# A two-layer hybrid encoder on one core: weight sums moved from VectorE to accumulating DMA, products of the MLP's first half in another order

## The chip, the core and the metric

The kernel runs on one core of a Trainium2 chip. Its engines work from queues of their own and wait for one another by semaphores: PE (TensorE) multiplies, DVE (VectorE) and ACT (ScalarE) do elementwise work, POOL (GpSimd) does a few small operations and issues DMA, and SP (SyncE) issues DMA. The metric is the time of one execution on the device, in microseconds.

## The reference

The reference is an encoder of two layers on one sequence of 512 positions with 1024 features, all in float32. Cut to what matters here:

```python
for l in range(DEPTH):
    xn = rms_norm(x, ln1[l])
    z = xn @ w_in[l]
    a_q, a_i, a_ff, a_fb, a_g, b_u, b_v, c_q, c_k, c_v, gz = jnp.split(z, offsets, axis=-1)
    ...   # branch A: gated scans; B: spatial gating; C: windowed attention
    merged = (gates[:, :, 0] * (y_a @ w_br[l, 0])
              + gates[:, :, 1] * (y_b @ w_br[l, 1])
              + gates[:, :, 2] * (y_c @ w_br[l, 2]))
    x = x + merged @ w_out[l]
    hn = rms_norm(x, ln2[l])
    x = x + jnp.square(jax.nn.relu(hn @ w_up[l])) @ w_down[l]
return rms_norm(x, final_norm)
```

`w_up` is 1024 x 4096 and `w_down` 4096 x 1024, in each layer.

## The kernel before

**Products in float32.** Every operand is split in two: `hi`, a cast of it, and `lo`, what the cast leaves. A product is three matmuls, hi by hi, hi by lo and lo by hi. For weights the cast runs on ACT (`wsplit`, L271, writes `wh`) and the rest is formed on DVE (L272, writes `wl`). Weights come in chunks of 128x1024, 512 KB. There are three buffers each of `wh` and `wl`, so a chunk can be split only when PE has finished with the chunk three places earlier. Activations are split in the same way (L336 on ACT, L337 on DVE).

**Seven products instead of eight.** The larger multiplications are cut into 2x2 blocks and done with seven block products, for which sums of weight blocks and sums of activation blocks are needed. A unit has seven products, each of two weight chunks, so fourteen splits. The blocks of a weight are called b11, b12, b22 and b21.

**The units of the MLP.** The hidden features are cut into four quarters (`qd`). For each quarter there is an `up` unit and then a `down` unit, a pair. Both run through `block_products`, in the order 1, 7, 6, 2, 5, 4, 3 (`ORDER`). The tile `t3` holds b12; b22 is added to it by an accumulating DMA issued by POOL (L261), for product 7. After that DVE adds b11 to it for product 6, and after product 6 it adds b21 for product 4 (both L548). b11 gets b12 by an accumulating DMA after product 7, for product 5. The result of product 1 is copied by ACT into a second pair of banks (`m`), so that product 2 accumulates on it there. The output of `up` goes through a squared ReLU and is split into halves 1 to 7 (`half`), the operands of the products of `down`. In `down`, DVE adds each result to the residual `xr` (L589). `down` adds `blks`, `blka` and `blkm`; `up` adds `blkc`, `blka` and `blkm`.

**The units ahead of attention.** Three units in each layer ("un") give one part of the columns of branches A and B and two gate projections. They run through `seven`, with loads by `uload` (L232) and weight sums on DVE alone: `early_sums` makes two sums of two chunks each (L462, L464), and `seven` two more before products 6 and 4 (L491). Their results go to the banks tA, tB, tC (first unit) and gA, gB, gC (the two others).

**Order.** A scheduler orders each engine's instructions from the order of the program; what stands under `hp()` goes ahead, and `issue_after` puts one instruction behind another. Loads of plain chunks go by SP's queue (L219, L232, L253), accumulating ones by POOL's (L261).

**The merge.** Ahead of the MLP the three branches are summed. One sum is written to DRAM and read back into `mB` by POOL (L1333); PE transposes another (mT, L1328), DVE adds the two (L1335), and the output projection "wo" follows. The first up and down units are loaded in this stretch.

**The change of layer.** After the last `down` of a layer, the row sums of squares are added (L414), scaled (L346, `ms`) and raised to the power −1/2 on POOL (L348, `rs`). PE spreads `rs` (L355, bc), DVE makes scales for the gates from it (L1000 to L1002), and PE goes on with the products "bu" (L277) while the first un unit is under way.

Of the kernel before, what the change touches and what calls it, by code (L numbers as in the profile page):

```python
# [6 lines left out]
F32 = mybir.dt.float32  # L7
# [71 lines left out]
def trunk(tc, x0v, xT, xt, ws, fnb, bsb, snk, wst, rope, cmask, amask, ident, out):  # L79
# [145 lines left out]
    def uload(*key):  # L225

        raw = []
        for q, tag in enumerate(("t3", "t3", "b22", "b21")):
            for i in range(2):
                t = W(tag)  # L230
                with hp():
                    d = nc.sync.dma_start(t, ws[CHUNK[key + (q, i)]])  # L232
                    if key == (0, "un", 0):
                        last_u[0] = d
                raw.append(t)
        return [raw[2 * q:2 * q + 2] for q in range(4)]

    class Unit:


        def __init__(self, *key):
            self.key, self.t = key, {}
# [4 lines left out]
        def load(self, what):  # L247
            q, tag = {"b11": (0, "wr"), "t3": (1, "t3"), "b22": (2, "b22"), "b21": (3, "b21")}[what]
            ts = self.t[what] = []
            for i in range(2):  # L250
                t = W(tag) if tag != "wr" else sb.tile([P, CW], F32, tag="wr", bufs=WR, name=nm("wr"))
                with hp():
                    nc.sync.dma_start(t, self.chunk(q, i))  # L253
                ts.append(t)
            if what == "t3":
                self.add("t3", 2)

        def add(self, what, q):
            with hp():
                for i in range(2):  # L260
                    nc.gpsimd.dma_start(self.t[what][i], self.chunk(q, i), accum_op=ALU.add)  # L261
# [195 lines left out]
    def early_sums(raw):  # L457
        b11, b12, b22, b21 = raw
        t1 = [part["G"].tile([P, CW], F32, tag="t1", bufs=2, name=nm("t1")) for _ in range(2)]
        raw.append(t1)  # L460
        for i in range(2):
            nc.vector.tensor_tensor(t1[i], b11[i], b12[i], ALU.add)  # L462
        for i in range(2):
            nc.vector.tensor_tensor(b12[i], b12[i], b22[i], ALU.add)  # L464

    def seven(raw, hs, name, on, order=(1, 2, 6, 7, 5, 4, 3), between=None, apart=False):

        b11, t3, b22, b21, t1 = raw
        V = nc.vector

        banks = {}
        use = {1: ("c", b11, "P1"), 2: ("m", b21, "P2"), 6: ("c", b11, "P16"), 7: ("a", t3, "P7"),
               5: ("c", t1, "P165"), 4: ("a", b21, "P74"), 3: ("c", b22, "P1653")}

        def mms(pt, p, k, xh, xl, hi, lo, c, start):
            t = slice(p * P, (p + 1) * P)
            o, h, l_ = by_two(pt), pairs(hi, c), pairs(lo, c)
            nc.tensor.matmul(o, xh[:, t], h, start=start and k == 0, stop=False, skip_group_check=True)
            nc.tensor.matmul(o, xl[:, t], h, start=False, stop=False, skip_group_check=True)
            return nc.tensor.matmul(o, xh[:, t], l_, start=False, stop=k == 3, skip_group_check=True)  # L480

        for n in order:
            tag, w, which = use[n]
            start = n in (1, 2, 7)
            if start:
                banks[tag] = [PT(tag, name + {"c": "A", "m": "B", "a": "C"}[tag]) for _ in range(2)]
            pts = banks[tag]
            with hp():
                for i in range(2):
                    if n == 6:  # L490
                        V.tensor_tensor(b11[i], t1[i], b22[i], ALU.add)  # L491
                    elif n == 4:
                        V.tensor_tensor(b21[i], b21[i], b11[i], ALU.add)
            split_w = []
            for s_ in range(2):
                with hp():
                    split_w.append(wsplit(w[s_]))
                if between and n == order[2] and s_ == 0:
                    third[0] = cast_i[0]
                if n == order[3] and s_ == 0 and waiting:  # L500
                    with tc.issue_after(cast_i[0].ins):
                        waiting.pop()()
                if not apart or n != order[-1]:
                    for k2 in range(2):
                        c = k2 * S
                        for p in range(2):
                            mms(pts[p], p, 2 * s_ + k2, *hs[2 * s_ + k2][n], *split_w[s_], c, start)
            for p in range(2):
                if apart and n == order[-1]:
                    with tc.issue_after(mm.ins) if p else contextlib.nullcontext():  # L510
                        for k in range(4):
                            c = (k % 2) * S
                            mm = mms(pts[p], p, k, *hs[k][n], *split_w[k // 2], c, start)
                with hp():
                    on(which, p, pts[p])
            if n == order[0] and between:
                between()

    ORDER = (1, 7, 6, 2, 5, 4, 3)
# [1111 lines left out]
```

## Time and profile before

| | |
|---|---|
| median of 3 runs | 1665.67 us (1663.78 to 1666.84) |
| profiled execution | 1663.91 us |
| its span | 1662.1 us |
| granted clock of PE, mean | 0.990 |
| PE busy | 1594.3 us, 96% |
| DVE busy | 1361.7 us, 82% |
| ACT busy | 1066.2 us, 64% |
| POOL busy | 183.7 us, 11% |
| accumulating DMAs issued by POOL | 64, of 512 KB each |

Times within the span count from its start. Layer 0 has its un units from about 43 to 157 us, the merge near 450, the four pairs from 507 to 824; layer 1 has the merge near 1285 and its pairs from 1340 to the end. In a row of a timeline stand the start, the duration, the engine, the line and the operation, then the tile written, an arrow and the tiles read; in brackets the idle time before it and what ended it. Instructions on one engine overlap by a little, so the step from start to start is shorter than the duration. In a row of waits stand who waits, for whom, and the total, the number and the longest.

### The profile page before, as it was taken

How to read it: one execution, taken by the hardware profiler on the slowest of the kernel's cores; microseconds unless marked ns; L12 is line 12 of the kernel's file. 1: busy time of each engine (PE TensorE's matmuls, PEld its weight loads, DVE VectorE, ACT ScalarE, POOL GpSimd, SP SyncE). 2: the span in 40 equal slices, each digit the busy share in tenths (PEclk: the TensorE clock that was granted, in tenths of full speed). 3: DMA queues.
4: the chain of work that ended last, by engine and by line, in shares of the span. 5: the costliest groups of instructions: out<-in, count | busy, mean ns of one | idle time of the engine just before them, and what ended most of it. 6: DMA issues, size and time to landing. Idle time of an engine off the chain costs nothing. (4 is left out here: it accounts for less than half of the span.)

```text
span 1662.1 us, 24573 instructions
## 1 busy us (share of the span) xinstructions
PE 1594.3 (96%) x9186; PEld 1423.4 (86%) x9186; DVE 1361.7 (82%) x2024; ACT 1066.2 (64%) x1815; POOL 183.7 (11%) x249
## 2 busy tenths in 40 slices
PE   9999999999899999999989999999999899999997
PEld 8888888998789897979778788888888798989796
DVE  7996998685468979797979869987955689797978
ACT  7576678775147666657655657687852377666575
POOL 1021001011310010000110211000103100100000
PEclk9999999999999999999989999999999999999999
DMA  9342222223854565754523522212228646667543
GB/s 344 102 152 96 86 77 67 86 96 101 264 199 140 153 181 144 188 151 136 182 71 115 177 89 82 77 51 96 96 86 254 230 129 164 176 152 190 152 112 83
DMA packets 66343, 229.57 MB, mean 138 GB/s; under 512 B 8528, under 2 KB 8912, under 8 KB 66224
## 3 DMA queue, kind: packets, MB, share of 16 engines
q1 hardware_dynamic: 45216, 156.03, 27.4%
q0 software_dynamic: 20864, 71.71, 17.6%
q8 instruction: 72, 1.18, 0.3%
q14 instruction: 47, 0.39, 0.1%
q10 hardware_dynamic: 144, 0.26, 0.0%
HBM read 209.10 MB, written 18.87 MB: 137 GB/s over the span
## 5 line engine op out<-in xcount | busy, mean ns | idle before, releaser
L272 DVE TENSOR_TENSOR wl<-wr,wh 128x1024 fp32r<-128x1024 f32 x166 | 202.2, 1220 | 85.7 <-ACT wh L271 85.0
L271 ACT CAST wh<-wr 128x1024 fp32r<-128x1024 f32 x166 | 173.1, 1044 | 147.4 <-PE yC L329 25.5
L271 ACT CAST wh<-t 128x1024 fp32r<-128x1024 f32 x146 | 152.7, 1046 | 109.1 <-PE blks L579 24.3
L272 DVE TENSOR_TENSOR wl<-t,wh 128x1024 fp32r<-128x1024 f32 x146 | 177.9, 1220 | 31.0 <-ACT wh L271 30.6
L272 DVE TENSOR_TENSOR wl<-b,wh 128x1024 fp32r<-128x1024 f32 x103 | 124.7, 1218 | 25.3 <-ACT wh L271 25.2
L271 ACT CAST wh<-b 128x1024 fp32r<-128x1024 f32 x103 | 107.1, 1045 | 55.8 <-PE blkc L608 13.1
L578 PE MATMUL blks<-wh,sh 128*128 128x512 f32 x256 | 99.0, 387 | 6.7 <-DVE xr L589 6.2
L580 PE MATMUL blks<-wl,sh 128*128 128x512 f32 x256 | 89.6, 387 | 9.7 <-DVE wl L272 9.7
L579 PE MATMUL blks<-wh,sl 128*128 128x512 f32 x256 | 97.6, 381 | 0.0
L807 DVE TENSOR_TENSOR ex<-ex 128x512 f32<-128x512 f32 x112 | 80.9, 740 | 2.7 <-ACT key L787 2.7
L337 DVE TENSOR_TENSOR sl<-u,sh 128x512 fp32r<-128x512 f32 x112 | 74.2, 681 | 1.7 <-ACT sh L336 1.6
L336 ACT CAST sh<-u 128x512 fp32r<-128x512 f32 x112 | 66.5, 616 | 13.3 <-DVE u L652 13.1
L765 PE MATMUL at<-qt,kt 128*128 128x128 f32 x448 | 66.5, 281 | 5.1 <-DVE qt L780 2.0
L609 PE MATMUL blkc<-xh,wl 128*128 128x256 f32 x256 | 70.0, 276 | 1.1 <-DVE wl L272 1.1
L608 PE MATMUL blkc<-xl,wh 128*128 128x256 f32 x256 | 69.8, 275 | 0.0
L607 PE MATMUL blkc<-xh,wh 128*128 128x256 f32 x256 | 69.6, 275 | 0.0
L765 PEld LDWEIGHTS at<-qt,kt 128*128 128x128 f32 x448 | 60.6, 195 | 7.8 <-issue 2.6
L580 PEld LDWEIGHTS blks<-wl,sh 128*128 128x128 f32 x256 | 48.8, 191 | 20.7 <-DVE wl L272 14.0
L578 PEld LDWEIGHTS blks<-wh,sh 128*128 128x128 f32 x256 | 48.7, 190 | 18.1 <-ACT wh L271 6.7
L261 POOL DMA_DIRECT2D wr<-in_ws_dram x32 | 27.8, 868 | 328.9 <-ACT sh L336 85.5
L779 ACT ACTIVATE qt<-ex 128x512 f32<-128x512 f32 x56 | 37.6, 671 | 35.3 <-DVE ex L807 25.1
L261 POOL DMA_DIRECT2D t<-in_ws_dram x32 | 27.6, 864 | 288.4 <-DMA t<-in_ws_dram 85.4
(464 smaller groups left out, 5409.7 us busy)
## 6 DMA issues: line engine op xcount, KB each, us to landing
wr<-in_ws_dram SPq DMA_DIRECT2D x134, 512.0 KB, 3.5
b<-in_ws_dram SPq DMA_DIRECT2D x91, 512.0 KB, 4.5
t<-in_ws_dram SPq DMA_DIRECT2D x58, 512.0 KB, 4.2
t<-in_ws_dram POOLq DMA_DIRECT2D x32, 512.0 KB, 8.9
wr<-in_ws_dram POOLq DMA_DIRECT2D x32, 512.0 KB, 5.6
thd<-zt POOLq DMA_DIRECT2D x32, 256.0 KB, 4.2
th<-thd POOLq DMA_DIRECT2D x32, 256.0 KB, 3.1
mgd<-mg POOLq DMA_DIRECT2D x16, 256.0 KB, 2.6
```

Of the source, the lines that this page charges most:

```text
L271: cast_i[0] = nc.scalar.copy(hi, raw)
L272: nc.vector.tensor_tensor(lo, raw, hi.bitcast(F32), ALU.subtract)
L336: nc.scalar.copy(hi, src)
L337: return nc.vector.tensor_tensor(lo, src, hi.bitcast(F32), ALU.subtract)
L578: nc.tensor.matmul(o, xh[:, t], h, start=start and k == 0, stop=False, skip_group_check=True)
L579: nc.tensor.matmul(o, xl[:, t], h, start=False, stop=False, skip_group_check=True)
L580: i = nc.tensor.matmul(o, xh[:, t], l_, start=False, stop=k == 3, skip_group_check=True)
L607: nc.tensor.matmul(o, hl[0][:, c], xh, start=start and k + j == 0, stop=False, skip_group_check=True)
L608: nc.tensor.matmul(o, hl[0][:, c], xl, start=False, stop=False, skip_group_check=True)
L609: i = nc.tensor.matmul(o, hl[1][:, c], xh, start=False, stop=k == 3, skip_group_check=True)
L765: nc.tensor.matmul(pt[:, c], kk(st), qq[:, c], start=True, stop=True)
L807: nc.vector.tensor_tensor(o_ap, o_ap, ap_of(ex, i_, [[istep, 2]] + z), ALU.add)
```

## The change

Five things are changed.

1. The un units use `block_products` as well (a new helper `by_token` gives the products). Their t3 is loaded as b12 and gets b22 by accumulating DMA; b11 gets b12 in the same way; product 1 goes by ACT into the banks of product 2. `uload`, `early_sums` and `seven` are gone. DVE makes two chunk sums in a unit instead of eight, and POOL issues six more accumulating DMAs.
2. In `down`, and in the un units, the third sum (t3 plus b21, after product 6) is an accumulating DMA. In `up` it stays on DVE.
3. `up` runs in the order 1, 7, 6, 4, 5, 2, 3. Halves 2, 5 and 3 are no longer split in `up`, but inside the following `down`, ahead of its products 6, 2 and 5 (`late`, `ahead`; in the last quarter all ahead of product 6).
4. In the first pair of a layer, the activation sums for `up` are made in two parts, `rest_of_x` ahead of product 4 and `last_of_x` ahead of product 2.
5. Loads of the next unit follow a table (`LOADS`) by kinds of units; the first un unit of layer 1 is loaded during the last `down` of layer 0. The accumulating DMAs of the first `up` of a layer are issued after the last load of mB (`behind`).

The core of the diff:

```diff
     class Unit:
-        def __init__(self, *key):
-            self.key, self.t = key, {}
+        def __init__(self, *key, behind=None):
+            self.key, self.t, self.behind = key, {}, behind
...
         def load(self, what):
-            q, tag = {"b11": (0, "wr"), "t3": (1, "t3"), "b22": (2, "b22"), "b21": (3, "b21")}[what]
+            q = {"b11": 0, "t3": 1, "b22": 2, "b21": 3}[what]
+            tag = what if what != "b11" else "t3" if self.key[1] == "un" else "wr"
...
         def add(self, what, q):
             with hp():
                 for i in range(2):
-                    nc.gpsimd.dma_start(self.t[what][i], self.chunk(q, i), accum_op=ALU.add)
+                    with tc.issue_after(self.behind[0].ins) if self.behind else contextlib.nullcontext():
+                        nc.gpsimd.dma_start(self.t[what][i], self.chunk(q, i), accum_op=ALU.add)
...
-    ORDER = (1, 7, 6, 2, 5, 4, 3)
+    LOADS = {("up", "dn"): {7: "t3", 2: "b21", 5: "b11", 3: "b22"}, ("dn", "un"): {7: "b11", 2: "b21", 4: "t3", 3: "b22"},
+             ("un", "un"): {5: "b11", 2: "b21", 4: "t3", 3: "b22"}}
+    LOADS["dn", "up"] = LOADS["up", "dn"]
-    def block_products(unit, chain, product, on, nxt=None, between=None, behind=None, apart=False):
+    def block_products(unit, chain, product, on, nxt=None, order=(1, 7, 6, 2, 5, 4, 3), between=None, inner=None, ahead={}, apart=False):
...
+            if n in ahead:
+                with hp():
+                    ahead[n]()
             for s_ in range(2):
                 with hp():
                     hl.append(wsplit(raw[s_]))
...
             with hp():
-                if n in (7, 6):
+                if n == 7 or n == 6 and unit.key[1] == "up":
                     for i in range(2):
                         V.tensor_tensor(w["t3"][i], w["t3"][i], w["b11" if n == 7 else "b21"][i], ALU.add)
                 if n == 7:
                     unit.add("b11", 1)
-            if nxt:
-                for what in {7: ("t3",), 2: ("b21",), 5: ("b11",), 3: ("b22",)}.get(n, ()):
-                    nxt.load(what)
+                elif n == 6 and unit.key[1] != "up":
+                    unit.add("t3", 3)
+            if n in loads:
+                nxt.load(loads[n])
...
             if which == "P12":
+                a11, a21, a22 = u[11, p], u[21, p], u[22, p] = T("u", "u"), u[21, p], u[22, p]
+                A.activation(nat(a11), srt(pt), AF.Relu)
+                square(a11)
+                marks.append(half(1, p, a11))
+                V.tensor_tensor(a21, a11, a21, ALU.subtract)
+                half(7, p, a21)
+                V.scalar_tensor_tensor(a11, a22, -1.0, a11, ALU.mult, ALU.subtract)
+                half(6, p, a11)
...
+        def late(n):
+            for p in range(2):
+                if n == 3:
+                    V.scalar_tensor_tensor(u[12, p], u[12, p], -1.0, u[11, p], ALU.mult, ALU.subtract)
+                half(n, p, u[12, p] if n in (2, 3) else u[22, p])
...
-        block_products(unit, "c", product, on, nxt, between, behind)
-        return hs, marks[0]
+        block_products(unit, "c", product, on, nxt, (1, 7, 6, 4, 5, 2, 3), between, ahead=ahead)
+        return hs, {6: lambda: late(2), 2: lambda: late(5), 5: lambda: late(3)}, marks[0]
...
-            if u == 0:
-                seven(raw, hx, "t", on_tok, (1, 7, 6, 2, 5, 4, 3), first_u if l else None)
-            else:
-                seven(raw, hx, "g", on_gate(u - 1), between=(lambda: head_0.extend(gates_0())) if u == early else None)
-            if nxt:
-                early_sums(nxt)
-            raw = nxt
+            block_products(unit, "csc"[u], by_token(hx), on_gate(u - 1) if u else on_tok, nxt, inner=inner)
+            unit = nxt
...
         def rest_of_x():
-            with hp():
-                for d in range(4):
-                    v_ = T("x", "xh", F32R), T("x", "xl", F32R)
-                    split(xf[d + 4], *v_)
-                    xo[d][2], xo[d][4] = two(v_, 0), two(v_, 1)
+            for d in range(4):
+                v_ = T("x", "xh", F32R), T("x", "xl", F32R)
+                split(xf[d + 4], *v_)
+                xo[d][2], xo[d][4] = two(v_, 0), two(v_, 1)
+
+        def last_of_x():
             for d in range(4):
                 sd = T("h", "sd")[:, 0:HT]
                 nc.vector.scalar_tensor_tensor(sd, xf[d + 4][:, 0:HT], -1.0, xa[d][:, HT:], ALU.mult, ALU.subtract)
...
-        unit = Unit(l, "up", 0)
+        unit = Unit(l, "up", 0, behind=last_m)
...
+            if qd == 3:
+                late = [ahead[n] for n in (6, 2, 5)]
+                ahead = {6: lambda: [f() for f in late]}
```

How this moves instructions shows at three places. First POOL's queue at the merge of layer 0. Before, the adds of both first units (t_1044 and t_1045 of up, t_1091 and t_1092 of down) stand ahead of the loads of mB:

```order
L261 DMA t_1044_4792<-in_ws_dram 128x1024
L261 DMA t_1045_4794<-in_ws_dram 128x1024
L261 DMA t_1091_4998<-in_ws_dram 128x1024
L261 DMA t_1092_5000<-in_ws_dram 128x1024
L1333 DMA mB_4250<-mgd 128x512
L1333 DMA mB_4262<-mgd 128x512
```

Afterwards two of them stand there, and the two of up (now t_1038 and t_1039) behind the last load of mB:

```order
L252 DMA t_1085_4988<-in_ws_dram 128x1024
L252 DMA t_1086_4990<-in_ws_dram 128x1024
L1276 DMA mB_4240<-mgd 128x512
L1276 DMA mB_4252<-mgd 128x512
...
L1276 DMA mB_4482<-mgd 128x512
L252 DMA t_1038_4782<-in_ws_dram 128x1024
L252 DMA t_1039_4784<-in_ws_dram 128x1024
```

So two transfers less stand ahead of the first mB; the two that moved are passed by twenty rows of exchanges and loads.

Second, DVE from the end of `up` into `down` in the third quarter of layer 0. Before, the sums of both kinds (L548) and the splits of all halves stand among the first weight splits of `down`:

```order
L272 TENSOR_TENSOR wl_7102<-t_1343_6625,wh_7101 128x1024
L337 TENSOR_TENSOR sl_6928<-u_6762,sh_6927 128x512
L548 TENSOR_TENSOR t_1344_6627<-t_1344_6627,wr_6827 128x1024
L337 TENSOR_TENSOR sl_6932<-u_6633,sh_6931 128x512
L337 TENSOR_TENSOR sl_6998<-u_4806,sh_6997 128x512
L548 TENSOR_TENSOR t_1343_6625<-t_1343_6625,b_1355_6751 128x1024
L589 SCALAR_TENSOR_TENSOR xr_4384<-blka_7055,r_1053_4809,xr_4384 128x512
L589 SCALAR_TENSOR_TENSOR xr_4386<-blka_7056,r_1053_4809,xr_4386 128x512
L272 TENSOR_TENSOR wl_7118<-t_1344_6627,wh_7117 128x1024
```

Afterwards only the first kind of sum is left (L488), and late splits (sl) follow the splits of product 6 (t) and of product 2 (b):

```order
L488 TENSOR_TENSOR t_1338_6617<-t_1338_6617,wr_6805 128x1024
L263 TENSOR_TENSOR wl_7074<-t_1337_6615,wh_7073 128x1024
L328 TENSOR_TENSOR sl_6914<-u_6900,sh_6913 128x512
L328 TENSOR_TENSOR sl_7066<-u_4796,sh_7065 128x512
L535 SCALAR_TENSOR_TENSOR xr_4374<-blka_7019,r_1047_4799,xr_4374 128x512
L263 TENSOR_TENSOR wl_7090<-t_1338_6617,wh_7089 128x1024
L328 TENSOR_TENSOR sl_7070<-u_4796,sh_7069 128x512
L535 SCALAR_TENSOR_TENSOR xr_4376<-blka_7020,r_1047_4799,xr_4376 128x512
L611 SCALAR_TENSOR_TENSOR u_4796<-u_4796,u_6883 128x512
L328 TENSOR_TENSOR sl_7110<-u_6621,sh_7109 128x512
L263 TENSOR_TENSOR wl_7118<-b_1363_6879,wh_7117 128x1024
```

Between the two splits of product 6 and the first of product 2 there stand now four splits and one sum of activations; the sums t,b are gone.

Third, DVE at the change of layer. Before, sums of the next un unit stand between the row statistics s and ms:

```order
L491 TENSOR_TENSOR t_1597_8191<-t_1609_8217,b_1601_8199 128x1024
L464 TENSOR_TENSOR t_1599_8195<-t_1599_8195,b_1601_8199 128x1024
L414 TENSOR_TENSOR s_1605_8207<-ss_1051_4807 128x4
L337 TENSOR_TENSOR xl_8037<-xf_8038,xh_8036 128x256
L491 TENSOR_TENSOR t_1598_8193<-t_1610_8218,b_1602_8201 128x1024
L464 TENSOR_TENSOR t_1600_8197<-t_1600_8197,b_1602_8201 128x1024
L272 TENSOR_TENSOR wl_8374<-wr_8371,wh_8373 128x1024
L346 TENSOR_SCALAR ms_8209<-s_1605_8207 128x4
```

Afterwards s and ms stand together behind the last residuals, one weight split and one activation split, and the scales gsc, which read rs, one weight split behind them:

```order
L535 SCALAR_TENSOR_TENSOR xr_4372<-blks_7766,r_1047_4799,xr_4372 128x512
L263 TENSOR_TENSOR wl_8310<-wr_8307,wh_8309 128x1024
L328 TENSOR_TENSOR xl_8026<-xf_8027,xh_8025 128x256
L405 TENSOR_TENSOR s_1599_8199<-ss_1045_4797 128x4
L337 TENSOR_SCALAR ms_8201<-s_1599_8199 128x4
L328 TENSOR_TENSOR xl_8035<-xf_8036,xh_8034 128x256
L263 TENSOR_TENSOR wl_8340<-wr_8337,wh_8339 128x1024
L949 TENSOR_SCALAR gsc_8265<-rs_8203 128x4
```

The sums have left this stretch.

More of the change, by code (lines that the diff above doesn't have):

```diff
@@ L455, in left_x @@
         return res
[L457 to L517, printed above, removed]
@@ L524, in block_products @@
         V, w = nc.vector, unit.t
         banks, turned = {}, None
+        loads = LOADS[unit.key[1], nxt.key[1]] if nxt else {}
         def open_(tag):
             banks[tag] = [PT(tag, "blk" + tag) for _ in range(2)]
-        for n in ORDER:
+        for n in order:
             tag = {2: "m", 7: "a", 4: "a"}.get(n, chain)
@@ L535, in block_products @@
             pts, hl = banks[tag], []
-            tail = apart and n == ORDER[-1]
+            tail = apart and n == order[-1]
+            if n in ahead:
+                with hp():
+                    ahead[n]()
             for s_ in range(2):
@@ L539, in block_products @@
                     hl.append(wsplit(raw[s_]))
+                if inner and n == order[2] and s_ == 0:
+                    third[0] = cast_i[0]
+                if n == order[3] and s_ == 0 and waiting:
+                    with tc.issue_after(cast_i[0].ins):
+                        waiting.pop()()
                 if not tail:
@@ L565, in block_products, with by_token @@
                         on(READ[n], p, pts[p])
-            if behind and n == 7:
-                behind()
-    def down(qd, unit, nxt, hs, xr, r2, nr2, done, last):
-        V = nc.vector
+    def by_token(hs):
         def product(n, pt, p, ks, hl, start):
@@ L581, in product, with down @@
             return i
+        return product
+    def down(qd, unit, nxt, hs, ahead, xr, r2, nr2, done, last):
+        V = nc.vector
         def on(which, p, pt):
@@ L591, in on, with up @@
                 done(t, fl)
-        block_products(unit, "s", product, on, nxt, apart=last and qd == 3)
-    def up(unit, nxt, xo, between=None, behind=None):
+        block_products(unit, "s", by_token(hs), on, nxt, ahead=ahead, apart=last and qd == 3)
+    def up(unit, nxt, xo, between=None, ahead={}):
         V, A = nc.vector, nc.scalar
@@ L640, in on @@
                 A.copy(nat(u[21, p]), srt(pt))
+            elif which == "P74":
+                t = u[21, p]
+                V.tensor_tensor(nat(t), nat(t), srt(pt), ALU.add)
+                A.activation(t, t, AF.Relu)
+                square(t)
             elif which == "P165":
@@ L994, in trunk @@
         if l == 0:
-            raw = uload(l, "un", 0)
-            early_sums(raw)
+            unit = Unit(l, "un", 0)
+            for what in ("b11", "t3", "b21", "b22"):
+                unit.load(what)
             boost[0] = True
@@ L1008, in on_tok @@
             lo_, hi_ = slice(p, p + 1), slice(2 + p, 3 + p)
[L1009 removed]
+            if which == "P12":
                 vt[p] = T("tv", "vt")
                 A.activation(vt[p], pt, AF.Copy, scale=rc[:, lo_])
[L1012 to L1013 removed]
             elif which == "P16":
@@ L1338, in turn_sum @@
             return pair
-        ms, summed = [None] * KT, [None]
+        ms, summed, last_m = [None] * KT, [None], [None]
         for fl in range(2):
@@ L1480, in trunk @@
             nxt = Unit(l, "dn", qd)
-            hs, mark = up(unit, nxt, xo) if qd else up(unit, nxt, xo, factors, rest_of_x)
+            hs, ahead, mark = up(unit, nxt, xo) if qd else up(unit, nxt, xo, factors, {4: rest_of_x, 2: last_of_x})
             if l == 0 and qd == 1:
@@ L1484, in trunk @@
                     lbs = lower_bounds()
-            unit, nxt = nxt, Unit(l, "up", qd + 1) if qd < 3 else None
+            unit, nxt = nxt, Unit(l, "up", qd + 1) if qd < 3 else None if last else Unit(l + 1, "un", 0)
             if qd == 3:
@@ L1490, in trunk @@
                         nc.sync.dma_start(fn_t[fl], bass.AP(tensor=fnb.tensor, offset=fnb.offset + fl * S, ap=[[0, P], [1, S]]))
-            down(qd, unit, nxt, hs, xr, r2, nr2, done, last)
+            if qd == 3:
+                late = [ahead[n] for n in (6, 2, 5)]
+                ahead = {6: lambda: [f() for f in late]}
+            down(qd, unit, nxt, hs, ahead, xr, r2, nr2, done, last)
             unit = nxt
-        if not last:
-            nxt = uload(l + 1, "un", 0)
         if not last:
```

60 lines of the change are left out of this document (16 added, 44 removed).

## The prediction

> **What bounds the kernel now.** I read the totals first, then what TensorE (PE) waits for, then the windows of single stages, and last the timelines of the places where a wait sits.
>
> ```profile
> span 1662.1 us, 24573 instructions
> PE 1594.3 (96%) x9186; PEld 1423.4 (86%) x9186; DVE 1361.7 (82%) x2024; ACT 1066.2 (64%) x1815; POOL 183.7 (11%) x249
> ```
>
> PE is busy 96% of the span and the change keeps every one of its products, so only the 67.8 us in which PE is not busy, and slow issue inside its busy time, can be won. The waits of PE, longest groups first:
>
> ```profile
> PE mT L1328 <- DVE mB L1335: 12.0, 2, 6.7
> PE blks L580 <- DVE wl L272: 9.7, 9, 1.6
> PE blks L578 <- DVE xr L589: 6.2, 8, 1.1
> PE blkm L579 <- DVE sl L337: 2.2, 5, 0.4
> PE gA L480 <- DVE wl L272: 2.2, 4, 1.0
> PE tC L480 <- DVE wl L272: 1.2, 1, 1.2
> ```
>
> Columns: total, times, longest. Four places carry the loss: the merge (mT), the hand-over from up to down in the eight MLP pairs (blks, blkm), the change of layer (its row comes below), and the seven-product units ahead of attention (gA, tC). I take them one by one. The eight pairs give 9.7 + 6.2 + 2.2 = 18.1 us of named waits.
>
> **A. The merge.** Here POOL issues four accumulating loads of the first MLP weights ahead of the loads of mB:
>
> ```profile
> 438.61 0.91 POOL L261 DMA_DIRECT2D t<-in_ws_dram  x1 [4.98 <-PE yA L330]
> 442.74 0.84 POOL L261 DMA_DIRECT2D t<-in_ws_dram  x1 [0.43 <-issue]
> 443.45 2.32 POOL L1333 DMA_DIRECT2D mB<-mgd  x4
> 447.13 0.54 POOL L1260 DMA_DIRECT2D th<-thd  x1 [1.37 <-DMA t<-in_ws_dram]
> ...
> 456.86 0.54 POOL L1260 DMA_DIRECT2D th<-thd  x1 [2.57 <-DMA t<-in_ws_dram]
> 458.34 0.54 POOL L1346 DMA_DIRECT2D mC<-mcd  x1 [0.95 <-DMA mB<-mgd]
> ```
>
> The first and the last of four th rows are shown; they are released by the landings of the four adds, so these land in turn, (456.86 − 447.13) / 3 = 3.24 us apart, and the first mB lands just behind the last. The change puts the two adds of the first up unit behind the last mB load; the two of the first down unit stay ahead. Two adds fewer are 6.5 us, so mB lands near 451.9 in layer 0. The wait there was 6.7 and in layer 1 it was 12.0 − 6.7 = 5.3. I take 1.2 and 1.5 us as left (landings jitter, and the first down's adds remain), so the gain is 5.5 + 3.8 = **9.3 us**. Bounds: 12.0 if nothing remains; 0 if what is left ahead costs as much as the four did. The moved adds pass the th, mC, xr and mB loads on POOL's queue, which all get earlier, and are needed when the first up begins near 507, some 40 us later, which covers them.
>
> **B. The change of layer.** DVE forms the early sums of the next unit between the last residuals and the row statistics:
>
> ```profile
> 824.60:842.80 18.20, 11.55 (x56) 9.19 (x55) 16.18 (x29) 12.80 (x32) 6.30 (x3) 0.78 0.34 116
> 831.69 0.15 DVE L414 TENSOR_TENSOR s<-ss 128x4 f32<-128x4 f32 x1
> 831.77 0.41 DVE L337 TENSOR_TENSOR xl<-xf,xh 128x256 fp32r<-128x256 f32 x1
> 832.10 1.21 DVE L491 TENSOR_TENSOR t<-t,b 128x1024 f32<-128x1024 f32 x1
> 833.24 1.21 DVE L464 TENSOR_TENSOR t<-t,b 128x1024 f32<-128x1024 f32 x1
> 835.51 0.16 DVE L346 TENSOR_SCALAR ms<-s 128x4 f32<-128x4 f32 x1
> 835.82 5.23 POOL L348 TENSOR_TENSOR rs<-ms,mhalf_t 128x4 f32<-128x4 f32 x1 [9.22 <-DVE ms L346]
> 841.10 2.08 PE L355 MATMUL bc<-id_t,rs 128*128 128x128 f32 x8 [4.13 <-POOL rs L348]
> ```
>
> The window row gives its length, then the busy time of PE, PEld, DVE, ACT, POOL: PE works 11.55 of 18.20 us. Six 128x1024 sums stand on DVE in this stretch (two each of L462, L464 and L491; two are shown), at 833.24 − 832.10 = 1.14 us back to back 6.8 us together; they leave DVE, and in the new order s and ms follow each other directly behind one wl and one xl. Then ms comes near 827.7 instead of 835.5; even with 5.23 us on POOL rs is there at 833, when PE is still at work on the bu products. I take the stretch at 12.2 us, its work plus 0.65, a gain of **6.0 us**. Bounds: 6.65 (no idle), and about 2 if gsc, which now stands one wl behind ms on DVE and waits for rs, holds the wl split behind it while POOL takes 5.23.
>
> **C. Six steady pairs.** One pair of up and down:
>
> ```profile
> 668.80:746.10 77.30, 74.68 (x506) 68.79 (x505) 66.03 (x75) 49.03 (x67) 6.92 (x8) 1.00 0.62 162
> 668.78 0.27 PE L607 MATMUL blkc<-x,wh 128*128 128x256 f32 x1
> 674.14 0.28 PE L607 MATMUL blka<-xb,wh 128*128 128x256 f32 x1
> ...
> 1382.95 0.22 PE blks L578
> 1388.13 0.43 PE blka L578 x2
> ```
>
> The starts of successive up products lie 5.36 us apart, those of an unhindered down product 5.18 (1388.13 − 1382.95, from the chain). Seven of each are 73.8 us, so a pair loses 77.3 − 73.8 = 3.5 us. PE's waits name 2.6 of it:
>
> ```profile
> PE blks L580 <- DVE wl L272: 1.6, 1, 1.6
> PE blks L578 <- DVE xr L589: 0.6, 1, 0.6
> PE blkm L579 <- DVE sl L337: 0.4, 1, 0.4
> ```
>
> All three end with DVE, whose timeline has no gap from 691 to 739; a part of it:
>
> ```profile
> 716.78 1.22 DVE L548 TENSOR_TENSOR t<-t,wr 128x1024 f32<-128x1024 f32 x1
> 717.91 1.28 DVE L337 TENSOR_TENSOR sl<-u,sh 128x512 fp32r<-128x512 f32 x2
> 719.12 1.22 DVE L548 TENSOR_TENSOR t<-t,b 128x1024 f32<-128x1024 f32 x1
> ...
> 725.58 1.22 DVE L548 TENSOR_TENSOR t<-t,b 128x1024 f32<-128x1024 f32 x1
> ```
>
> The two t,b sums of down become DMA: 2 × 1.14 = 2.3 us less in the stretch that paces. The new order of up moves its fourth product, with one sum and its activation, out of the tail, and the splits for halves 2, 5 and 3 (six at (719.12 − 717.91) / 2 = 0.60 us, and two sums) behind the weight splits of P6, P2 and P5. Going through the new order by hand with these durations I find only the first wl of P2 late, by 1.0, with 0.3 of small waits: 1.3 left of 3.5, against 2.2 gained; I take 2.1. Six pairs (quarters 1 to 3 of both layers) give **12.6 us**. Bounds: 0 (the work only moved) to 6 × 3.5 = 21. Up's P4 now follows P6 and splits the sum made between; the rows of that place cost it at nothing:
>
> ```profile
> 679.29 1.22 DVE L548 TENSOR_TENSOR t<-t,b 128x1024 f32<-128x1024 f32 x1
> 680.71 1.22 DVE L272 TENSOR_TENSOR wl<-b,wh 128x1024 fp32r<-128x1024 f32 x1 [0.20 <-ACT wh L271]
> 683.35 1.23 DVE L272 TENSOR_TENSOR wl<-b,wh 128x1024 fp32r<-128x1024 f32 x1 [1.41 <-ACT wh L271]
> ```
>
> The sums already stand there, done by 680.5, and DVE idles 1.4 us before each split: the cover. Without it the sum would cost its 1.14 us per up.
>
> **D. The two first pairs.** They lose more early and as much late, but there the eight small operations of last_of_x move behind into the full stretch (8 × 0.33 = 2.6 us, by 832.10 − 831.77 of the 128x256 row above). I put them at **0**, ±1.5 each.
>
> **E. Units ahead of attention.** DVE makes eight 128x1024 sums per unit now, two afterwards, 6.8 us less; P1 and P2 leave through one bank, one ACT copy more and one DVE addition less. The gA and tC waits of the first list are 2.2 + 1.2 = 3.4 us. I take the whole, **3.4 us** (0 to 3.4).
>
> **F. New waits for DMA.** Where DVE summed, PE's next split now waits for POOL's queue: 36 more adds in the six units and 16 in the eight downs. What an add costs today:
>
> ```profile
> L261 POOL DMA_DIRECT2D t<-in_ws_dram x32: 841/862/907, 438.6 to 1572.0; - x32
> ...
> DMA to landing us min/median/max: 5.4/6.9/13.8
> ```
>
> In a down the add of the third sum can be issued when P6 is split, some 13 us in, and P4, sixth in order, is split from 5 × 5.18 − 2 = 24 us on. 13 + 6.9 is 20, with the worst of today 27: 4 us of slack, or 3 short. Between two units t3 is loaded at P4, then added to; it is wanted at P7 of the next unit. A plain load of 512 KB takes 3.7 at the median (the loads of L253):
>
> ```profile
> DMA to landing us min/median/max: 3.3/3.7/10.8
> ```
>
> 24 + 3.7 + 6.9 = 34.6, one more add in the queue 3.2, 37.8, against 7 × 5.18 + 5.18 − 2 = 39.4. That is tight, but enough. An add waits on POOL until its buffer is free, and behind it wait that queue's other adds and its exchanges for the gates, which have the slack of a unit or more. I take **0**, bounds 0 and 2 us per unit (28 in fourteen units).
>
> [...]
>
> **The sum.** 9.3 + 6.0 + 12.6 + 0 + 3.4 − 0 = 31.3 us. The profiled execution took 1663.9 us, 1.8 more than its span; it becomes 1632.6. The median of the runs shown, 1665.7, is 1.8 above it, hence **1634 us**.
>
> **Rivals.**
>
> *DVE still paces the pairs* (18%). It keeps all weight splits and the moved activation splits; if the late splits push P2's wl as far as the sums did, C is 0: 1634 + 12.6 = 1646. For it speaks the gapless DVE; against it, that work leaves for good.
>
> *The merge still waits* (13%). The first down's two adds are ahead, and if they too are issued late, or mB's slots come free late, A is 0: 1643.
>
> *The sums by DMA land too late* (12%; slower than before in about 6, even in 2). PE's cast of a summed half waits, ACT's queue stands behind it, and the wh and wl of the following halves with it. Each microsecond of lateness costs 14 us over fourteen units; it cancels the gain from 31.3 / 14 = 2.2 us per unit on, that is landings near 14 us in downs instead of 7. At 3 us it gives 1634 + 42 = 1676. The maximum of 13.8 speaks for it, the medians against.
>
> *The change does not do what it says* (5%): late splits or the ACT copies of P1 open a wait as long as the one that closes, everything but A is lost, and it ends at 1666 − 9 = 1657, or within no change if A also fails.
>
> **How the numbers follow.** The forecast holds 52%; its own range is 1624 to 1645 (C from 4 to 18, F up to 4). The range for 8 in 10 takes in the first two rivals: 1621 to 1653. What a measurement here can tell from no change is 0.2%, 3.3 us. Faster: 52 + 18 + 13 + 4 from each of the last two, 91, less 3 for two rivals at once: 0.88. Same 0.05, slower 0.07.
>
> **What would show it.** In the new profile mT's wait for mB should be under 3 us in total; bc should not wait for rs; a steady pair should take 75 to 76 us; gA and tC should not wait for wl. A PE or ACT wait for "DMA t" or "DMA wr" of over 1 us in a unit refutes F, a pair of 77 us refutes C.

## The result, and the profile after

The changed kernel takes 1635.64 us at the median (1632.5 to 1636.66), against 1664.79 us (1663.78 to 1666.84) for the kernel before, run beside it: a ratio of 0.982, with a 95% interval of 0.9802 to 0.9838. The forecast was 1634 us. The whole came out almost as said; its parts did not, and they are what this section and the experiments are about.

First the totals of the changed kernel, in the same form as before.

```profile
span 1632.9 us, 24646 instructions
PE 1591.0 (97%) x9186; PEld 1430.2 (88%) x9186; DVE 1301.4 (80%) x1960; ACT 1067.5 (65%) x1819; POOL 226.4 (14%) x301
```

The span is 29.2 us shorter. DVE lost 60 us of work and POOL gained 43, and PE, with the same 9186 matmuls, is busy 97% of the time. Now what PE waits for (total, times, longest):

```profile
PE blkc L553 <- ACT xb L327: 4.7, 2, 2.3
PE yB L268 <- DVE gz L893: 3.7, 2, 2.6
PE xT L392 <- ACT u L399: 3.5, 1, 3.5
PE blkc L519 <- ACT wh L262: 2.9, 1, 2.9
PE blkm L521 <- DVE wl L263: 2.8, 1, 2.8
PE mT L1271 <- DVE mB L1278: 1.1, 3, 0.4
```

The old list was led by 12.0 us at mT and 18.1 us at the hand-over from up to down. Here mT is down to 1.1, the hand-over is all but gone from the list, and five waits stand there that did not exist or were small. One row of a window shows how far the steady pair went:

```profile
1402.90:1476.80 73.90, 73.90 (x506) 69.22 (x505) 64.16 (x73) 48.75 (x67) 8.73 (x10) 1.00 0.70 180
```

PE is busy for 73.90 us of 73.90: the pair is at the length of its matmuls, against 77.30 before. Cutting both timelines at the same events of PE gives the account of the whole. Each number is a length in us, before and after:

| stretch | layer 0 | layer 1 | change, both | forecast |
|---|---|---|---|---|
| merge, first mT to first wo (A) | 14.5 → 8.0 | 13.1 → 7.7 | −12.0 | −9.3 |
| end of layer 0's pairs until bu runs through (B) | | 18.1 → 12.2 | −5.9 | −6.0 |
| six steady pairs (C) | 234.4 → 224.0 | 232.1 → 221.7 | −20.7 | −12.6 |
| first pair (D) | 82.8 → 82.1 | 81.1 → 82.0 | +0.2 | 0 |
| un units, the rest of their stretch (E, F) | 125.9 → 126.6 | 157.1 → 158.6 | +2.2 | −3.4 |
| attention, first at to first mT | 276.0 → 278.6 | 280.1 → 283.4 | +5.9 | 0 |
| output projection, first wo to the first up | 47.7 → 48.2 | 47.7 → 48.1 | +0.9 | 0 |
| start and tail | | | +0.3 | 0 |

The sum is −29.2 (−29.1 by the rounded entries). The two large terms were too small by 11 us together, and about 13 us were lost in places to which the forecast gave nothing or a gain.

### The profile page after: what moved, and what is told of

It is laid out like the page before. It is cut to its first block, busy times and chain, and to the rows that moved or that the text cites. A ratio compares the mean times of both kernels' runs of the same rounds, so it can differ in the third digit from the quotient of the medians.

```text
span 1632.9 us, 24646 instructions
## 1 busy us (share of the span) xinstructions
PE 1591.0 (97%) x9186; PEld 1430.2 (88%) x9186; DVE 1301.4 (80%) x1960; ACT 1067.5 (65%) x1819; POOL 226.4 (14%) x301
## 4 chain that ended last, share of the span: by engine, by line
PE 70%; DVE 11%; ACT 7%; issue 6%; DMA 4%; POOL 1%; SPq 0%; POOLq 0%; DVEq 0%; ACTq 0%
PE blkc L554 4%; PE blkc L555 4%; PE blkc L553 4%; PE blks L521 4%; PE blks L520 3%; PE blks L519 3%; PE blka L519 3%; PE blka L520 2%; PE blka L521 2%; DVE wl L263 2%; DVE ex L755 2%; PE blka L553 2%; PE blka L555 2%; PE blka L554 2%; ACT wh L262 1%
## 5 line engine op out<-in xcount | busy, mean ns | idle before, releaser
L263 DVE TENSOR_TENSOR wl<-t,wh 128x1024 fp32r<-128x1024 f32 x158 | 192.3, 1221 | 62.6 <-ACT wh L262 61.9
L262 ACT CAST wh<-t 128x1024 fp32r<-128x1024 f32 x158 | 165.3, 1047 | 110.4 <-PE blks L520 23.7
L262 ACT CAST wh<-b 128x1024 fp32r<-128x1024 f32 x91 | 95.0, 1044 | 55.2 <-PE blka L554 12.3
L252 POOL DMA_DIRECT2D t<-in_ws_dram x84 | 75.7, 903 | 377.2 <-DMA t<-in_ws_dram 163.6
L263 DVE TENSOR_TENSOR wl<-b,wh 128x1024 fp32r<-128x1024 f32 x91 | 111.1, 1221 | 19.3 <-ACT wh L262 18.5
L519 PE MATMUL blks<-wh,sh 128*128 128x512 f32 x256 | 95.2, 384 | 0.6 <-ACT sh L327 0.6
L519 PEld LDWEIGHTS blks<-wh,sh 128*128 128x128 f32 x256 | 48.2, 191 | 7.3 <-ACT sh L327 1.1
```

What stands on the lines that cost most here:

```text
L262: cast_i[0] = nc.scalar.copy(hi, raw)
L263: nc.vector.tensor_tensor(lo, raw, hi.bitcast(F32), ALU.subtract)
```

## The experiments

The times of whole kernels below are medians; the kernel before was run again beside each group (1664.4 to 1664.8 us), and ratios are to it. Lengths of stretches and waits are from one profiled execution of each build.

### The hand-over: the sum by DMA alone, and the order alone

The kernel before, with one part of the change:

```diff
-                if n in (7, 6):
+                if n == 7 or n == 6 and unit.key[1] == "up":
...
                 if n == 7:
                     unit.add("b11", 1)
+                elif n == 6 and unit.key[1] != "up":
+                    unit.add("t3", 3)
```

> The kernel before, with one edit: the third weight sum of each down (t3 plus b21) is made by two accumulating DMAs instead of two DVE sums. Theory (the length of DVE's work at the hand-over from up to down sets the pair, so 2 x 1.14 = 2.3 us off DVE are 2.3 us off the pair): a steady pair, 77.3 us in the kernel before and 73.9 in the changed one, takes 75.0; six of them and about 1.2 in each first pair give 1664.8 - 16 = 1649 us. Rival A (the sums were not what PE waited behind; the late splits and the new order of up carry the gain): 76.8 to 77.3 per pair, 1661 to 1665 us. Rival B (the adds land too late and PE's P4 waits): over 77.3.

And the changed kernel with this part undone in down, the order of up and the late splits kept:

```diff
-                if n == 7 or n == 6 and unit.key[1] == "up":
+                if n == 7 or n == 6 and unit.key[1] != "un":
...
-                elif n == 6 and unit.key[1] != "up":
+                elif n == 6 and unit.key[1] == "un":
```

> The changed kernel, with the third weight sum of each down back on DVE; the order of up and the late splits stay. Theory (every microsecond on DVE at the hand-over counts): a steady pair takes 75.0 to 76.0 us against 73.9, the whole 1635.6 + 8 x 1.1 to 2.1 = 1644 to 1652 us. Rival A (order and late splits alone carry the gain): 73.9, 1636 us. Rival B (only the sum by DMA carries it): 77.3, 1636 + 8 x 3.4 = 1663 us.

The first takes 1647.87 us (ratio 0.9903, 0.9887 to 0.992), the second 1648.23 (0.9903, 0.9883 to 0.9922). A steady pair of each, in the view of windows (length, then busy time of PE, PEld, DVE, ACT, POOL); first the kernel before with the sum by DMA:

```profile
1412.70:1487.70 75.00, 74.42 (x506) 68.84 (x504) 63.74 (x73) 49.05 (x67) 8.66 (x10) 1.00 0.73 181
```

Then the changed kernel with the sum on DVE:

```profile
1414.00:1489.50 75.50, 74.66 (x506) 69.00 (x505) 66.28 (x75) 48.82 (x67) 7.01 (x8) 1.00 0.65 164
```

DVE's busy time differs by two operations of 1.2 us, and the pair goes from 77.3 to 75.0 where only they are taken off: exactly their 2.3 us. So DVE's length at the hand-over did set the pair, and both rivals of both runs fall: a pair takes neither 73.9 us nor 77. The order and the late splits are worth 77.3 − 75.5 = 1.8 on their own. Both together win 3.4, less than 2.3 + 1.8 = 4.1, because 3.4 to 3.5 is all that a pair had to lose. The second run's profiled execution is 16.7 us longer than that of the changed kernel, and its eight pairs explain 10.7; the remainder lies at the merge, to which the experiments come back.

### The merge: the adds of up back in front

```diff
-        unit = Unit(l, "up", 0, behind=last_m)
+        unit = Unit(l, "up", 0)
```

> The changed kernel, with the two adds of the first up ahead of the loads of mB again. Theory (each add ahead keeps mB back by its 3.2 us): PE waits 12 us at mT again in both layers together, against 1.1 now, and the time is 1635.6 + 11 = 1647 us. Rival (what kept mB was the first two adds alone, or something else moved): mT's wait stays under 3 us, 1636 to 1638 us.

It takes 1646.96 us (0.9894, 0.9879 to 0.9908), and PE's longest wait is the old one:

```profile
PE mT L1271 <- DVE mB L1278: 13.2, 2, 7.0
```

The position of these two adds is worth 13.2 − 1.1 = 12.1 us of waiting, and 11.3 us of time.

### The units ahead of attention as before

All of the change but its first point: the un units with their weight sums on DVE again (`uload`, `early_sums` and `seven` of the kernel before, and with them the later load of layer 1's first un unit), MLP and merge as changed.

> The changed kernel, with the units ahead of attention made as before (all their weight sums on DVE, no accumulating DMA in them); MLP and merge as changed. In the changed kernel the stretch from the first at to the first mT is longer than before by 2.6 us in layer 0 and 3.3 in layer 1, the un units of layer 0 are longer by 0.7, and the stretch from the end of layer 0's pairs to the first at of layer 1 is shorter by 4.4. Theory (all of this comes with the new un units): attention is back at 276.0 and 280.1 us, the other two stretches as before, 1635.6 - 0.7 - 5.9 + 4.4 = 1633.5 us. Rival (the longer attention has nothing to do with the un units, the scheduler moved it for other reasons): 1635.6 - 0.7 + 4.4 = 1639 us.

It takes 1634.53 us (0.9822, 0.9807 to 0.9837). Attention is back at 276.0 us in layer 0 and 280.8 in layer 1, the un units of layer 0 at 126.3, and layer 1 from the end of the pairs to its first at is 175.1 us, as before the change (175.2), against 170.8. So the longer attention comes with the new un units, and as a whole the largest part of the diff moved the time by less than 0.1%: what it wins at the change of layer it gives back. What lengthens layer 0's attention shows in the last experiment. For layer 1 it was not settled; PE's largest new wait there is that of yB for DVE's gz, 2.6 us, in the list above.

### Gate writes and tables off POOL's queue

In the un units of layer 0 PE waits 2.9 us for ACT, and in those of layer 1 2.8 us for DVE. The timelines of the changed kernel say why. ACT first:

```profile
108.86 1.03 ACT L262 CAST wh<-b 128x1024 fp32r<-128x1024 f32 x1
117.37 0.69 ACT L988 ACTIVATE zt<-blkm,gsc 128x512 f32<-128x512 f32 x1 [7.48 <-DMA thd<-zt]
117.96 1.03 ACT L262 CAST wh<-t 128x1024 fp32r<-128x1024 f32 x1
```

The tanh of L988 has no free buffer zt until a gate tile has been written to DRAM, and the cast of the next weights stands behind it on ACT. On POOL that write follows an add:

```profile
108.58 0.90 POOL L252 DMA_DIRECT2D t<-in_ws_dram  x1 [3.31 <-ACT zt L994]
109.17 1.44 POOL L979 DMA_DIRECT2D thd<-zt  x2
```

It was issued at 109.17 and let ACT go at 117.37, 8.2 us later, where the writes took 4.0 at the median. In layer 1 it is DVE:

```profile
910.34 0.69 DVE L1097 TENSOR_TENSOR cos<-cos,rb 128x512 f32<-128x512 f32 x1 [2.53 <-DMA cos<-in_rope_dram]
...
912.14 1.22 DVE L263 TENSOR_TENSOR wl<-b,wh 128x1024 fp32r<-128x1024 f32 x1
```

DVE waits for a small table, the weight split stands behind, and PE behind that. The gate writes and the layer's four small tables were moved to other queues (of the tables, bsb is not shown):

```diff
-                nc.gpsimd.dma_start(thd[:, i * 4 + t, fl * S:(fl + 1) * S], z)
+                nc.scalar.dma_start(thd[:, i * 4 + t, fl * S:(fl + 1) * S], z)
...
-        nc.gpsimd.dma_start(wst_t, wst[l])
+        nc.sync.dma_start(wst_t, wst[l])
...
-        nc.gpsimd.dma_start(cos_t, rope[:, 0])
-        nc.gpsimd.dma_start(sin_t, rope[:, 1])
+        nc.sync.dma_start(cos_t, rope[:, 0])
+        nc.sync.dma_start(sin_t, rope[:, 1])
```

> The changed kernel, with the gate tiles written to DRAM by ACT's queue and four small tables of each layer (wst, bsb, cos, sin) loaded by SP's queue; before both went by POOL's queue, among the accumulating adds. In the changed kernel a gate write issued right behind an add landed 8.1 us later, ACT's tanh waited 7.5 us for it and PE 2.9; in layer 1 cos landed 8.0 us after its issue behind an add, DVE waited 2.5 us for it and PE 2.8; after both PE's granted clock was near 0.5 for 3 to 4 us. Theory (transfers issued by POOL stand behind its adds): both waits of PE go, 2 x 4.4 us, 1635.6 - 9 = 1627 us. Rival A (the DMA engines are full, whoever issues): the writes still land 7 to 8 us after issue, 1635 us. Rival B (issuing costs ACT as much as it gains, or SP's loads are kept back): 1633 us or more, the waits replaced by others on ACT.

It takes 1627.77 us (0.9786, 0.9766 to 0.9806), and yet the theory holds in one place only. In layer 1 SP's queue issued cos at 888.7, long before its use, PE's wait for DVE there is gone, and the stretch to the first at goes from 170.8 to 166.0. In layer 0 the write, now issued by ACT, is as late as ever:

```profile
107.97 0.94 ACTq L979 DMA_DIRECT2D thd<-zt  x2
108.95 1.05 ACT L262 CAST wh<-b 128x1024 fp32r<-128x1024 f32 x1 [0.40 <-ACT zt L994]
115.64 0.69 ACT L988 ACTIVATE zt<-blkm,gsc 128x512 f32<-128x512 f32 x1 [5.64 <-DMA thd<-zt]
```

From 107.97 to 115.64 are 7.7 us. There rival A is right: changing the queue did not help (7.7 us instead of 8.2). What is under way at the same time is the likely cause (an add issued at 107.95 landed at 117.47, a plain load issued at 108.94 at 117.65, and from 109 to 119 the mean busy share of the DMA engines is 0.93 to 1.03). The un units of layer 0 stay at 126.6 us. That the total met the theory's 1627 us is therefore luck: in the profiles the stretch before layer 1's attention won 4.8 us, that attention 1.7 and the first pairs 2.0, while the merges lost 4.4.

### The first pair: activation sums one product earlier

PE's wait for xb stands at product 3 of the first up. What it costs shows in the granted clock, the third number from the end of a window's row. The changed kernel:

```profile
527.00:541.00 14.00, 11.90 (x107) 11.71 (x105) 11.88 (x17) 11.86 (x19) 1.55 (x2) 1.00 0.96 282
...
543.20:546.00 2.80, 2.57 (x12) 2.49 (x12) 2.80 (x7) 0.57 (x1) 0.00 (x0) 0.50 0.04 15
546.00:548.40 2.40, 2.40 (x14) 2.40 (x13) 1.72 (x4) 1.15 (x3) 0.00 (x0) 0.50 0.00 0
548.40:550.00 1.60, 1.60 (x15) 1.60 (x15) 1.56 (x3) 1.58 (x2) 0.00 (x0) 0.95 0.00 0
```

PE stood still for 2.3 us up to 541.2; its clock was 0.63 over the next 2 us (not shown) and then 0.50 until 548.4. The edit:

```diff
-            hs, ahead, mark = up(unit, nxt, xo) if qd else up(unit, nxt, xo, factors, {4: rest_of_x, 2: last_of_x})
+            hs, ahead, mark = up(unit, nxt, xo) if qd else up(unit, nxt, xo, factors, {4: rest_of_x, 5: last_of_x})
```

> The changed kernel, with last_of_x ahead of product 5 of the first up instead of product 2. In the changed kernel PE waits 2.3 us for xb at the first product 3, and the granted clock is 0.5 from 541 to 548. Theory (the activation sums are late where they stand, and DVE has idle time of 1.4 us per split earlier; what the wait costs is the wait and about 3.5 us of slow clock behind it): the first pairs take 77 us instead of 82.1, 1635.6 - 10 = 1626 us. Rival A (the wait goes, but DVE is full and the next wl is late by as much): 82 us, 1636. Rival B (only the wait itself is won): 1635.6 - 2 x 2.7 = 1630 us.

The first pairs take 78.1 and 78.2 us instead of 82.1 and 82.0, one microsecond more than the theory had: about 1.1 us of waits for wl and wh are left. It is more than the wait alone (2.7 each, rival B), so the slow clock is part of the price: in layer 0's first pair PE's busy time for the same 522 matmuls fell from 79.31 to 76.98 us and its clock rose from 0.96 to 1.00. The time is 1630.74 us (0.9801, 0.9784 to 0.9818), 4.9 below the changed kernel where two pairs won 7.8: this build's mT waits 4.1 us in all, and 3 us went there.

### A sum without lead: up's third sum by DMA too

```diff
-                if n == 7 or n == 6 and unit.key[1] == "up":
+                if n == 7:
...
-                elif n == 6 and unit.key[1] != "up":
+                elif n == 6:
```

> The changed kernel, with the third weight sum of up made by accumulating DMA too. There product 4 follows product 6 directly, so the add has the 5.36 us of one product between the split of product 6 and its use, less the 2.3 us of cast and wl. Theory (an add takes at least 5.4 us to land, so it comes 2.4 us or more too late, and PE's clock falls behind the wait): 8 ups x 2.4 to 6 us, 1655 to 1684 us. Rival (the adds come in time, as they do in down, where three products lie between): 1634 to 1637 us, steady pairs 73.9.

It takes 1655.78 us (0.9943, 0.9921 to 0.9965), 20 us worse than the changed kernel, at the lower end of the theory. Who waits for the accumulating DMAs (total, times), in the changed kernel:

```profile
  ACT wh L262: 4.5, 2
```

And with up's sum among them:

```profile
  ACT wh L262: 50.3, 20
```

So the slower case that was priced in the prediction exists: it is a matter of the distance between the product after which the sum is made and the one that needs it. Where the use comes three products later (down) no cast waits; where it comes in the very next product (up) a steady pair takes 75.1 to 78.3 us. The two waits of 4.5 us in all stand in the un units.

### All adds behind the merge

The mT wait was 1.1 us in the changed kernel's profile, but 7.0 with down's sum on DVE, 4.3 with the old un units, 4.9 with other queues and 4.1 with the earlier sums, none of which touches the merge. With one profiled execution of each, builds and executions are not told apart. The adds of the first down were still ahead of mB.

```diff
-            nxt = Unit(l, "dn", qd)
+            nxt = Unit(l, "dn", qd, behind=None if qd else last_m)
```

> The changed kernel, with the adds of the first down behind the last load of mB too. PE's wait at mT was 1.1 us in the profile of the changed kernel, but 7.0 and 4.3 in two variants in which nothing near the merge was edited. Theory (the two adds left ahead keep mB back by an amount that differs between builds and executions): mT's wait under 0.5 us, 1635.6 - 1 to 3 = 1633 us. Rival (mB waits for its own transfers by now): no change, 1635 to 1636 us. Rival B (four adds behind make the first up wait for t3): PE or ACT waits for t in the first up, over 1637 us.

It takes 1627.32 us (0.978, 0.9765 to 0.9794): more than the theory allowed. mT no longer stands among the waits, and from the merge on PE does not pause:

```profile
448.00:505.00 57.00, 57.00 (x298) 50.47 (x297) 36.92 (x56) 25.80 (x45) 13.75 (x23) 1.00 0.68 214
```

From the first mT to the second pair it saves 4.8 us in layer 0 and 3.3 in layer 1. Most of it is in the output projection (44.9 us instead of 48.2: 1.3 less idle time of PE and 2.0 less busy time), where PE had waited for mB and mC; the theory had looked at mT alone.

### Three moves together, and the want of buffers

The last three runs have the adds behind mB, last_of_x ahead of product 5 and the tables on SP's queue. The second of them has two more buffers:

```diff
-             "xs": 16, "zt": 6,
+             "xs": 16, "zt": 8,
```

The third has the un units of the kernel before.

> The changed kernel with three moves at once: the adds of the first down behind the last load of mB too, last_of_x ahead of product 5, and the four small tables of each layer loaded by SP's queue (the gate writes stay on POOL's). Theory (three places that do not touch one another): the gains add, 8 us from the adds, 7.8 from the two first pairs (82.1 to 78.1 each, as measured alone), 4.8 from the un units of layer 1: 1635.6 - 20.6 = 1615 us. Rival (they compete for the same DMA time or DVE time): 1622 us or more.

> As the run with three moves, with eight buffers for the gate tiles (zt) instead of six. A gate write landed 7.7 to 8.1 us after its issue whether POOL or ACT issued it, since adds and plain loads were under way with it; ACT's tanh had no free buffer meanwhile. Theory (the wait in layer 0's un units is a want of buffers): PE's wait of 2.9 us there goes with the slow clock behind it, 4 us less than the run with three moves, 1611 us. Rival (ACT then waits for the next thing that is late, the weight sum t of the next product): the wait moves by a few us, 1614 to 1616 us.

> The run with three moves, with the units ahead of attention made as before (weight sums on DVE). It asks what the new un units are worth once their side effects are gone. Theory (they gain at the change of layer and lost it to late tables and a longer attention; with the tables early a part remains): 1618 to 1621 us against 1615. Rival (the new un units are worth nothing or less): 1613 to 1615 us.

They take 1615.42 us (0.9708, 0.9695 to 0.9722), 1609.78 (0.9678, 0.9664 to 0.9692) and 1619.84 (0.9735, 0.9722 to 0.9748). The three gains add up as forecast. The two buffers are worth 5.6 us more, and the kernel with them is the fastest of all, 25.9 us below the changed one. A gate write issued at 109.72 lands even later there, more than 9 us after its issue, but no ACT instruction waits for a zt any more: it had hurt by a want of buffers.

That is only part of the gain, though. In the profiles 4.0 us are won from the first un product to the first mT of layer 0, and 2.6 of them lie in attention, which takes 276.0 us as in the kernel before instead of 278.6. PE's 1522 matmuls there stand again in the order of the kernel before; in every other build with the new un units they stand in another order, and attention takes 278.5 to 278.7. So the longer attention of layer 0 came with another order of PE's instructions, which the two buffers undo. Layer 1's keeps the new order and takes 282.8 us, against 280.1 before.

The third run says that, beside the three moves, the new un units are worth 4.4 us, which they did not show at first, although attention is still longer with them (278.6 and 283.4 us against 276.1 and 281.2).

What PE still waits for in the fastest kernel:

```profile
PE yB L268 <- DVE gz L893: 3.5, 2, 2.6
PE xT L392 <- ACT u L399: 2.9, 1, 2.9
PE pT L1189 <- ACT yc L1196: 1.9, 2, 1.6
```

## Why the prediction was right, and where it was not

**A, the merge: mechanism right, term too small.** Forecast 9.3 us, measured 12.0, and 11.3 by putting the adds back. The failed step is "I take 1.2 and 1.5 us as left": in this build 1.1 was left in all. Across the builds 1.1 to 7.0 were left, so the residue was real, and that the profile after is at the good end of it is luck.

**B, the change of layer: right in size, for reasons partly other.** 12.2 us was forecast for the stretch and 12.2 measured. As said, s and ms come early and bc no longer waits. But POOL's rs took 1.09 us, not the 5.23 on which the bound rested. What followed it in the kernel before:

```profile
841.08 0.17 DVE L1000 TENSOR_SCALAR gsc<-rs 128x4 f32<-128x4 f32 x1 [0.93 <-POOL rs L348]
```

And the changed kernel:

```profile
813.66 0.17 DVE L337 TENSOR_SCALAR ms<-s 128x4 f32<-128x4 f32 x1
...
813.98 1.09 POOL L339 TENSOR_TENSOR rs<-ms,mhalf_t 128x4 f32<-128x4 f32 x1 [1.49 <-DVE ms L337]
814.70 1.22 DVE L263 TENSOR_TENSOR wl<-wr,wh 128x1024 fp32r<-128x1024 f32 x1 [0.53 <-ACT wh L262]
```

In the kernel before, rs began among back-to-back splits and sums of DVE and ended 0.9 us after the last of them; in the changed kernel DVE paused at 814.17, before its next split, and rs ended 0.9 us later as well. The four builds with DVE's early sums in this stretch have 4.89 to 5.23 us for rs, the nine others 1.09 to 1.11. So the 5.23 were probably a wait of POOL for DVE and no cost of the operation; no run isolates this.

What was not seen is a new wait: ACT's cast of a bu weight waits for its load, the activation u, for which xT waits, stands behind it on ACT, and PE loses 3.5 us at xT (second fence of the result).

```profile
819.32 1.04 ACT L262 CAST wh<-wr 128x1024 fp32r<-128x1024 f32 x1 [1.47 <-DMA wr<-in_ws_dram]
```

**C, the steady pairs: mechanism right, term too small.** Forecast 2.1 us a pair, measured 3.45, the whole loss. The failed step is the walk through the new order by hand, which left P2's first wl 1.0 us late; in the profile PE waits for nothing there. The two single-part runs show that the 2.3 us of the sums were fully on the path and that the order adds 1.8. The rival that DVE still paces the pairs is refuted by PE's 73.90 of 73.90. The rows given for the cover of up's sum show idle times of 0.2 and 1.4 us, not 1.4 before each split; the sum cost PE nothing all the same.

**D, the first pairs: 0 forecast, +0.2 measured, but not for the reason given.** The waits at the hand-over went, and the wait for xb (2.3 us in each layer) with its clock of 0.50 took their place. The step that put 2.6 us of moved work into the full stretch named the right place and the wrong price: what was late was not the next split but an operand of PE itself.

**E, the un units: wrong.** Forecast −3.4 us, measured +2.2. The waits of gA and tC for summed weights went, as said, but two longer ones came: blkc for ACT, 2.9 us, and blkm for a wl that DVE made late, 2.8 us, each with its stretch of slow clock (0.52 over 3 us, 0.57 over 4 us).

**F, the new waits for DMA: the step that failed.** That the sums themselves land in time was right for the downs, and in the un units it held to within 4.5 us of ACT's waiting. But "its exchanges for the gates, which have the slack of a unit or more" was false: a gate write that takes 4.0 us at the median took 8.1 where adds and loads were under way, and the buffers it holds have no such slack. The same goes for the tables (in layer 1 cos landed 8.0 us after its issue, and DVE waited 2.5 us for it). By the profiles of the runs that took them away, the late tables cost 4.8 us and the want of buffers 4.0, of which 2.6 are the other order in layer 0's attention. The attention's 5.9 us in both layers, which comes with the new un units, was in no term. In the rival on late sums, landings "near 14 us" should read 24 − 13 + 2.2 = 13.2.

**The sum.** It came right by luck: 11 us too little in A and C met about 13 us of losses that were not forecast. The 52% case is thus confirmed by its total and in A, B and C by its mechanisms, while its terms E and F failed. Of the rivals, the late sums were shown to exist only where a sum has no lead. The range held. Of the signs named at the end, mT under 3 us and no wait of bc for rs came, and the pair went below the 75 to 76 us named. The un units still have a wait for wl, and ACT waited twice for accumulated chunks, 4.5 us in all, which by the sign set there refutes F.

## What to carry to other kernels

Here, moving DVE's sums to DMA paid the full length of that work where DVE was on the path (2.3 us of a pair, 77.3 to 75.0), and little or nothing was given back where the sum is used three products after it is made (no cast waited in the downs); where the next product uses it, it cost more than it won (1655.78 us against 1635.64). The price was paid by neighbours: a gate write landed 8.1 us after its issue instead of 4.0, a table after 8.0. So count what else is in flight with the new transfers (small tables, spills, buffers held until a write lands), and give these more lead or another buffer. A wait of two or three microseconds on TensorE (2.3 us at xb) was followed by a clock of 0.50 in the changed kernel and is to be priced with that risk, and a critical load should not stand behind bulk transfers, even where one profile shows it in time (with adds ahead of mB the wait at mT was 1.1 us in one build and 7.0 in another).

## What the runs showed of the hardware

A pause of PE of 2.3 us (with two shorter ones of 0.3 and 0.2 right behind it) was followed by a granted clock of 0.50 for at least 5.2 us (543.2 to 548.4), so the same matmuls of 128x256 started 0.21 us apart instead of 0.11; after the pause of 2.9 us in the un units the clock was 0.52 over the next 3 us and 1.00 after that. Not every such pause was followed by a slow clock: the wait of 2.6 us at yB in layer 1 was followed by 0.54 over 3.7 us in the changed kernel and by 1.00 in the fastest one (mean clock over the span 0.989 and 0.998), and a wait of 3.0 us at blkm by 1.00 in the run with the adds back in front.

At one place a transfer landed late whichever queue issued it: the gate write of 256 KB landed 8.1 us after its issue from POOL and 7.7 from ACT, against medians of 4.0 and 4.1 over all 32 gate writes.

The issue of an accumulating DMA took about as long with 116 of them as with 64. In the changed kernel:

```profile
L252 POOL DMA_DIRECT2D t<-in_ws_dram x84: 854/875/2057, 32.9 to 1600.9; - x84
```

The median of 875 ns stands against 862 before; a single issue took 2057.
